# PSUM sums and accumulating DMAs in the second product of an MLP by Strassen-Winograd

## The chip, the cores and the metric

One core of a Trainium2 chip runs the kernel. The metric is the device time of one execution in microseconds (us); the median of several runs is given. The engines are TensorE (PE, with its weight loads PEld), VectorE (DVE), ScalarE (ACT), GpSimd (POOL) and SyncE (SP), which issues the DMAs before the change. SBUF is the on-chip memory, PSUM the memory in which TensorE accumulates, in banks of 128 x 512 float32.

## The reference

A trunk of two layers over x, 1024 tokens of 1024 channels, float32. Each layer has a token mixer (layer 0 a recurrent block, layer 1 a pooling mixer) and an MLP, both gated and modulated by a conditioning vector c:

```python
for i in range(DEPTH):
    sh_m, sc_m, gt_m, sh_f, sc_f, gt_f = split(silu(c) @ w_mod[i] + b_mod[i])
    x = x + gt_m * mixer_i(rms_norm(x) * (1 + sc_m) + sh_m)
    h = rms_norm(x) * (1 + sc_f) + sh_f
    u = relu(h @ w1[i])                  # 1024 -> 4096
    x = x + gt_f * ((u * u) @ w2[i])     # 4096 -> 1024
return rms_norm(x)
```

## The kernel before

The channels lie on the partitions, eight blocks of 128, and the tokens in two halves of 512: `x[h][:, k, :]` is block k of half h, in SBUF (`xa`, `xb` in the profile). Every product is made of three matmuls of 128 x 128 by 128 x 512 (`mm3`, lines 178 to 180): both operands are split into a high and a low part, which add up to float32.

The MLP of a layer runs in eight chunks of 512 hidden channels. `f1` makes a chunk's hidden channels: eight products of 24 matmuls, each followed by relu and square on ScalarE, casts there and subtractions on VectorE. `f2_fast` makes the second product, from Winograd's form of Strassen's method: W2.T is cut into two by two blocks for each of four row blocks r (rows r and r + 4 of the output), the hidden channels into two by two as well, and seven products of six matmuls replace eight. Their operands are sums: of weights, made by `f2_weights` on VectorE one row block ahead (raw tile `raw_w`; parts `w_a_a`, `w_a_s`, `w_s_s`, `w_s`), and of hidden channels (`t1` to `t4`, `ut` in the profile).

`f2_fast` is called whole for twelve chunks: 0 to 5 of layer 0 and 1 to 6 of layer 1, which are written (i, c) here. Chunk (0,6) calls it twice with part of the products, (1, 5, 6, 3, 7) and (2, 4). The rest of the chunks uses the ordinary product, `f2_block`.

What becomes of the products of row block r, with g the gate's column, and the four blocks of the output named by (row, half):

- 1 goes to all four. `S.copy` (line 789) brings it to SBUF (`c1`), and `scaled` (line 774, ScalarE) makes g x product 1, which GpSimd adds to (0,0) (`add_scaled`, line 779).
- 5 goes by `add` (line 770, VectorE, out of PSUM) to (0,1) and (1,1), 2 to (0,0), 3 to (0,1), 4 to (1,0).
- 6 is added to `c1` by VectorE (line 800); ScalarE scales the sum (line 774), GpSimd adds it to (0,1).
- 7 is added on top (line 804), scaled, and added by GpSimd to (1,0) and (1,1).

So a row block has 7 operations on VectorE, 4 on ScalarE and 4 on GpSimd, 52 row blocks with the four of chunk (0,6).

Each product has its own PSUM bank from a pool of six (`acc_mm`), so the bank of a product comes free for the sixth after it. Work tiles (`tmp`) circulate in seven buffers, raw weights in three, split weights in eight. Instructions of an engine run in the order of its queue; a scheduler decides that order when the kernel is built, and waits between engines are set by the data. In layer 0 a step of the conditioning (`drip`, line 197: a product of a loaded tile `mb` with `cond` on VectorE) is taken with each unit of weights.

Of the kernel before, what the change touches and what calls it, by code (L numbers as in the profile page):

```python
# [15 lines left out]
P = 128  # L16
# [10 lines left out]
W = PAD + H  # L27

# Columns of the packed per-channel vectors, eight columns (one per block of channels) each.
# [13 lines left out]
def trunk_kernel(ctx, tc, xT, vecs, wmod, w_k, w_in, w_y, w_g, w_out, w_p, w1, w2, outT):  # L43
# [16 lines left out]
    class Blocks:  # L60
        """Eight blocks of channels of one half of the tokens, in two slots"""
# [41 lines left out]
    # The weights of the first products, in the order in which they are used: two blocks of rows  # L103
    # of six blocks of the input projection, and the conditioning's blocks of columns.
    mod_raw, k_raw = {}, []

    def piece(r, q, part):
        """Columns of a part of r, which is halved for the first two blocks of rows."""
        n = r.shape[-1] // (2 if q == 0 else 1)
        return part * n, part * n + n  # L110
# [29 lines left out]
    # silu(c) as a row on every partition  # L140
    cs = const.tile([P, NB], F32, name="cs")
    with tc.issue_after(S.activation(cs, vcol("c"), AF.Sigmoid).ins):
        # has the table of the first norm's square root loaded ahead of it
        S.activation(const.tile([P, 1], F32, name="early"), eps, AF.Sqrt)
# [3 lines left out]
    for n in range(2):  # L148
        ps = small_ps()
        # the columns of cs on diagonals, whose sums over the partitions are on every partition  # L150
# [23 lines left out]
    def mm3(ps, unit, col, rh, rl, first, last):  # L174
        """ps += unit[:, col:col+128].T @ (rh + rl)"""
        w, c = unit[col // H], col % H
        wh = w[:, 0, c:c + P]
        PE.matmul(out=ps, lhsT=wh, rhs=rh, start=first, stop=False)  # L178
        PE.matmul(out=ps, lhsT=wh, rhs=rl, start=False, stop=False)  # L179
        PE.matmul(out=ps, lhsT=w[:, 1, c:c + P], rhs=rh, start=False, stop=last)  # L180

    def proj(unit, hh, hl):
        """One 128-row block of W.T @ h for one token half, K = 1024."""
# [11 lines left out]
    def mod_column(m, e, raw):  # L195
        """m[:, e] = raw @ cond"""
        V.scalar_tensor_tensor(raw, raw, 1.0, cond, op0=ALU.mult, op1=ALU.mult, accum_out=m[:, e:e + 1])  # L197
# [8 lines left out]
    def mod_steps():  # L206
        """The rest of the conditioning in small steps, taken between those of the other work."""
# [19 lines left out]
    def norm_scale(g, m, name):  # L227
        """g * (1 + scale)"""
# [5 lines left out]
    class SumSq:  # L234
        """Sums of squares of n tokens: up to three partial sums, added up by the tensor engine."""
# [19 lines left out]
    def rstd_bcast(ss, trace=None):  # L255
        """PSUM tile [P, n] with 1/sqrt(mean + eps) of every token on every partition."""
# [10 lines left out]
        # in two float32r parts on diagonals, whose sums over the partitions are on every partition  # L267
# [38 lines left out]
    # Six blocks of the input projection take the channels of the first half of the tokens  # L306
    # as the conditioning of each 128 of them is ready.
# [8 lines left out]
    def after(f, *args, **kw):  # L316
        """Issues behind what the last call on the same engine issued."""
# [7 lines left out]
    def column(dst, j, k, scale, first):  # L325
        """dst[:, k] = first + scale * (conditioning of channel block k)"""
# [16 lines left out]
    def prepare(q, part=0):  # L343
        """The float32r parts of the weights of two blocks of rows, or of one if q is 0"""
# [126 lines left out]
    # coefficient of the gate in log a: 8 * log_sigmoid(lambda)  # L471
# [17 lines left out]
    # log1p(z) = 2 s (1 + po)  # L489
# [11 lines left out]
    def gates(hd, unit, h):  # L501
        """RG-LRU of one head; its states take the place of its input."""
# [16 lines left out]
        for mi in range(2):  # L519
            b = 2 * hd + mi  # L520
            # a = exp(log a);  1 - a^2 = (1 + a^2) * tanh(-log a)
# [77 lines left out]
    # U[c]: the hidden channels of chunk c, in slots of two blocks each: (first or last two blocks,  # L599
    # half of the tokens), and the sums of them that the second product of the MLP takes  # L600
# [3 lines left out]
    def f1_block(unit, j, h, u, fast):  # L604
# [7 lines left out]
        def minus(a, n):  # L612
            """a less a block that is there in its two parts"""
# [15 lines left out]
        # for f2_fast the halves of the tokens change places  # L629
# [33 lines left out]
    class Ahead:  # L663
        """Units of weights, which are prepared one ahead of those in use"""
# [11 lines left out]
    # pieces of the conditioning by unit of a chunk of the MLP  # L676
# [35 lines left out]
    def f2_weights(i, c, r, eng=None):  # L712
        """The parts of blocks of rows r and r + 4 of W2.T for f2_fast, by the product that takes them"""
# [399 lines left out]
```

## Time and profile of the kernel before

| | |
|---|---|
| median of 3 runs (1795.46 to 1798.61) | 1798.42 us |
| the profiled execution: its span | 1797.3 us |
| TensorE busy | 1718.5 us, 96% |
| VectorE | 1419.8 us, 79% |
| ScalarE | 913.7 us, 51% |
| GpSimd | 585.9 us, 33% |
| DMA queues | one, hardware_dynamic: 157.43 MB, 26.9% of 16 engines' span; two of instructions below 1% |

Only the span is known of the profiled execution, and the rows below have their times from its start. A row of a timeline gives the start, the duration, the engine, the line, the operation with what it writes and reads, and behind "[" the idle time of the engine ahead of it and what ended it. Matmuls overlap: one lasts 0.39 us and the next starts 0.23 us after it did. VectorE's operations overlap a little as well. Lines in the profile are those of the kernel before; the first lines of the changed kernel's functions lie 3 to 16 further down.

### The profile page before, as it was taken

The numbers are of one execution on the slowest core, as the hardware profiler recorded it, in microseconds if no ns is written. First come the engines' busy times: TensorE is split into PE (matmuls) and PEld (weight loads), VectorE is DVE, ScalarE is ACT, GpSimd is POOL, SyncE is SP. The second block draws the span as 40 slices with busy tenths as digits, with TensorE's granted clock in tenths as the row PEclk, the third lists the DMA queues.
The fourth block names the chain that finished last, engine by engine and source line by source line (L and its number), as shares of the span: only waits on it lengthen the run. The fifth ranks groups of instructions, "written<-read, shape, count | busy, mean of one in ns | idle before, by whom it ended". The sixth has DMA issues, their size and how long they took to land.

```text
span 1797.3 us, 20872 instructions
## 1 busy us (share of the span) xinstructions
PE 1718.5 (96%) x7510; PEld 1405.2 (78%) x7510; DVE 1419.8 (79%) x2124; ACT 913.7 (51%) x1558; POOL 585.9 (33%) x434
## 2 busy tenths in 40 slices
PE   6899989989999999999999988999999999999997
PEld 4687768778788888888888766788887787878787
DVE  8997866678888889898876897958787878686836
ACT  4588884255454444545454464445444444545422
POOL 5323341242322414151324655511322324041403
PEclk8999989989999999999999988999999999999999
DMA  9223314521424233242213221231202111121202
GB/s 363 73 84 109 136 47 142 162 83 59 136 70 134 73 115 106 94 126 73 83 58 106 81 72 59 83 105 51 70 33 71 36 59 52 42 61 46 71 13 94
DMA packets 47479, 158.76 MB, mean 88 GB/s; under 512 B 5008, under 2 KB 7440, under 8 KB 47376
## 3 DMA queue, kind: packets, MB, share of 16 engines
q1 hardware_dynamic: 47376, 157.43, 26.9%
q8 instruction: 59, 0.97, 0.2%
q14 instruction: 44, 0.36, 0.1%
HBM read 153.21 MB, written 4.19 MB: 88 GB/s over the span
## 4 chain that ended last, share of the span: by engine, by line
PE 62%; DVE 22%; ACT 5%; issue 5%; DMA 4%; POOL 2%; DVEq 0%; SPq 0%; ACTq 0%; POOLq 0%
PE mm L178 20%; PE mm L179 20%; PE mm L180 20%; DMA mb<-in_wmod 3%; DVE mb L197 2%; DVE xa L770 1%; DVE mw L323 1%; POOL xa L779 1%; DVE pw L900 1%; DVE xb L770 1%; DVE xca L439 1%; PE sm L262 1%; DVE hl L291 1%; DVE w_a_s L171 1%; DVE xcb L439 1%
## 5 line engine op out<-in xcount | busy, mean ns | idle before, releaser
L178 PE MATMUL mm<-hh,w_w 128*128 128x512 f32 x1024 | 401.4, 392 | 0.9 <-DVE xa L770 0.9
L180 PE MATMUL mm<-hh,w_w 128*128 128x512 f32 x1024 | 400.9, 392 | 0.0
L179 PE MATMUL mm<-hl,w_w 128*128 128x512 f32 x1024 | 400.6, 391 | 0.0
L779 POOL TENSOR_TENSOR xb<-xb,c 128x512 f32<-128x512 f32 x104 | 150.4, 1446 | 632.1 <-ACT c L774 564.4
L178 PEld LDWEIGHTS mm<-hh,w_w 128*128 128x128 f32 x1024 | 193.5, 189 | 42.8 <-DVE xa L770 2.7
L180 PEld LDWEIGHTS mm<-hh,w_w 128*128 128x128 f32 x1024 | 193.6, 189 | 40.3
L179 PEld LDWEIGHTS mm<-hl,w_w 128*128 128x128 f32 x1024 | 193.5, 189 | 40.0
L779 POOL TENSOR_TENSOR xa<-xa,c 128x512 f32<-128x512 f32 x104 | 160.3, 1542 | 145.1 <-ACT c L774 145.1
L774 ACT ACTIVATE c<-c,mod 128x512 f32<-128x512 f32 x104 | 75.3, 724 | 209.7 <-DVE c L800 119.8
L197 DVE SCALAR_TENSOR_TENSOR mb<-mb,cond 128x1024 f32<-128x1024 f32 x80 | 113.8, 1423 | 55.2 <-DMA mb<-in_wmod 54.6
L620 ACT ACTIVATE relu<-mm 128x512 f32<-128x512 f32 x128 | 76.2, 595 | 152.4 <-PE mm L180 143.6
L170 ACT CAST w_w<-raw_w 128x512 fp32r<-128x512 f32 x192 | 113.5, 614 | 63.2 <-PE mm L180 50.6
L171 DVE TENSOR_TENSOR w_w<-raw_w,w_w 128x512 fp32r<-128x512 f32 x136 | 130.5, 967 | 16.8 <-ACT w_w L170 16.7
L770 DVE SCALAR_TENSOR_TENSOR xa<-mm,mod,xa 128x512 f32<-128x512 f32 x156 | 112.9, 741 | 16.6 <-POOL xa L779 16.6
L171 POOL TENSOR_TENSOR w_w<-raw_w,w_w 128x512 fp32r<-128x512 f32 x56 | 83.5, 1498 | 71.6 <-ACT w_w L170 62.6
L179 PE MATMUL mm<-u,w_w 128*128 128x512 f32 (+1 forms) x224 | 81.4, 363 | 1.7 <-DVE u L610 1.7
L178 PE MATMUL mm<-u,w_w 128*128 128x512 f32 (+1 forms) x224 | 80.8, 364 | 1.7 <-ACT u L609 1.7
L180 PE MATMUL mm<-u,w_w 128*128 128x512 f32 (+1 forms) x224 | 81.0, 362 | 0.0
L178 PE MATMUL mm<-u,w_a_a 128*128 128x512 f32 x200 | 79.1, 396 | 1.9 <-DVE xa L770 1.0
L610 DVE TENSOR_TENSOR u<-usq,u 128x512 fp32r<-128x512 f32 x102 | 72.9, 715 | 8.5 <-ACT u L609 7.5
L770 DVE SCALAR_TENSOR_TENSOR xb<-mm,mod,xb 128x512 f32<-128x512 f32 x104 | 77.0, 741 | 2.6 <-PE mm L180 2.2
L179 PE MATMUL mm<-u,w_a_a 128*128 128x512 f32 x200 | 78.0, 390 | 0.0
(332 smaller groups left out, 4078.3 us busy)
## 6 DMA issues: line engine op xcount, KB each, us to landing
raw_w<-in_w SPq DMA_DIRECT2D x148, 512.0 KB, 3.6
mb<-in_wmod SPq DMA_DIRECT2D x80, 512.0 KB, 3.6
mw<-in_wmod SPq DMA_DIRECT2D x16, 512.0 KB, 9.6
raw_in<-in_w_in SPq DMA_DIRECT2D x8, 512.0 KB, 3.7
raw_y<-in_w_y SPq DMA_DIRECT2D x8, 512.0 KB, 3.6
raw_o<-in_w_out SPq DMA_DIRECT2D x8, 512.0 KB, 3.7
outT<-o SPq DMA_DIRECT2D x12, 256.0 KB, 2.4
xa<-in_xT SPq DMA_DIRECT2D x4, 512.0 KB, 5.4
```

The costliest lines, as they stand in the source:

```text
L170: S.copy(w[:, 0, 0:n], raw)
L171: (eng or V).tensor_sub(w[:, 1, 0:n], raw, w[:, 0, 0:n].bitcast(F32))
L178: PE.matmul(out=ps, lhsT=wh, rhs=rh, start=first, stop=False)
L179: PE.matmul(out=ps, lhsT=wh, rhs=rl, start=False, stop=False)
L180: PE.matmul(out=ps, lhsT=w[:, 1, c:c + P], rhs=rh, start=False, stop=last)
L197: V.scalar_tensor_tensor(raw, raw, 1.0, cond, op0=ALU.mult, op1=ALU.mult, accum_out=m[:, e:e + 1])
L439: V.scalar_tensor_tensor(o, xr[:, k:k + H], vcol(f"cw{k}", m), o, op0=ALU.mult, op1=ALU.add)
L610: eng.tensor_sub(u[n][:, 1, jj, :], src, u[n][:, 0, jj, :].bitcast(F32))
L620: S.activation(r, ps, AF.Relu)
L770: V.scalar_tensor_tensor(xb, ps, g[:, r + 4 * row:r + 4 * row + 1], xb, op0=ALU.mult, op1=ALU.add)
L774: S.activation(t, src, AF.Identity, scale=g[:, r + 4 * row:r + 4 * row + 1])
L779: G.tensor_add(xb, xb, t)
```

## The change

Products that go to the same outputs are summed in PSUM. In a row block, product 2 is accumulated onto the bank of 1, product 3 onto that of 5, and product 7 onto that of 6, without clearing it. The bank is read once before the second product (1, 5 and 6 are needed alone) and once after it. So a row block uses four banks in place of seven.

- Product 1: ScalarE scales it twice out of PSUM, by the gate of row 0 and of row 1 (tiles `c1[r][0]`, `c1[r][1]`). No copy.
- Product 5 is added to (1,1) only; when 3 has been accumulated onto it, 5 + 3 goes to (0,1).
- Product 6: VectorE makes g0 x 6 + `c1[r][0]` (line 815); 6 + 7 then makes g1 x (6 + 7) + `c1[r][1]` (line 820). Both are scaled already.
- 1 + 2 goes to (0,0), as `add` of product 2.

The scaled sums reach x by `nc.gpsimd.dma_start(xb, t, accum_op=ALU.add)` (line 788), a DMA of 128 x 512 from SBUF to SBUF that adds onto its destination: three for a row block, 144 in all. The two partial calls of chunk (0,6) share banks (3 onto 5, 7 onto 6) and keep GpSimd's additions (line 790), 16 in all. In row blocks 1 to 3 of the whole calls the order of the products is 1, 5, 6, 4, 3, 7, 2, in row block 0 it stays 1, 5, 6, 3, 7, 2, 4.

```diff
-        def product(parts, n):
-            ps = acc_mm()
+        def product(parts, n, onto=None):
+            ps = acc_mm() if onto is None else onto
             w, c0, ops = parts[n]
             for k in range(2):
-                mm3(ps, [w], c0 + k * P, u[ops][:, 0, k, :], u[ops][:, 1, k, :], k == 0, k == 1)
+                mm3(ps, [w], c0 + k * P, u[ops][:, 0, k, :], u[ops][:, 1, k, :],
+                    onto is None and k == 0, k == 1, True)
             return ps
...
         def add_scaled(t, r, row, col):
             xb = x[1 - col][:, r + 4 * row, :]
-            G.tensor_add(xb, xb, t)
+            if whole:
+                nc.gpsimd.dma_start(xb, t, accum_op=ALU.add)
+            else:
+                G.tensor_add(xb, xb, t)
...
-            ps = product(units[r], n)
+            ps = banks[r, n] = product(units[r], n, banks.get((r, {2: 1, 3: 5, 7: 6}.get(n))))
             if n == 1:
-                c1[r] = tmp("c1")
-                S.copy(c1[r], ps)
-                add_scaled(scaled(ps, r, 0), r, 0, 0)
+                c1[r] = [scaled(ps, r, row) for row in (0, 1)]
+                if not whole:
+                    add_scaled(c1[r][0], r, 0, 0)
+                    c1[r][0] = c1[r][0], tmp("c")
             elif n == 2:
                 add(ps, r, 0, 0)
             elif n == 5:
-                add(ps, r, 0, 1)
                 add(ps, r, 1, 1)
             elif n == 3:
                 add(ps, r, 0, 1)
+                if whole:
+                    add_scaled(c1[r][0], r, 0, 1)
             elif n == 6:
-                w = w16[r] = c1[r]
-                V.tensor_add(w, ps, c1[r])
-                add_scaled(scaled(w, r, 0), r, 0, 1)
+                src, w = (c1[r][0], c1[r][0]) if whole else c1[r][0]
+                V.scalar_tensor_tensor(w, ps, gate(r, 0), src, op0=ALU.mult, op1=ALU.add)
+                if not whole:
+                    add_scaled(w, r, 0, 1)
             elif n == 7:
-                w = w16[r]
-                V.tensor_add(w, ps, w)
-                c = scaled(w, r, 1)
-                add_scaled(c, r, 1, 0)
-                add_scaled(c, r, 1, 1)
+                w = c1[r][1]
+                V.scalar_tensor_tensor(w, ps, gate(r, 1), w, op0=ALU.mult, op1=ALU.add)
+                if (r, 4) in banks or not whole:
+                    add_scaled(w, r, 1, 0)
+                add_scaled(w, r, 1, 1)
             else:
                 add(ps, r, 1, 0)
+                if whole and (r, 7) in banks:
+                    add_scaled(c1[r][1], r, 1, 0)
...
-            for n in products:
+            for n in products if r == 0 or not whole else (1, 5, 6, 4, 3, 7, 2):
                 step(r, n)
```

The scheduler puts the instructions in a new order at three places of which the prediction speaks. `mm_...` are PSUM banks by product, `ut2` and `ut4` are the operands of products 6 and 4, `u11` that of 3.

TensorE, chunk (1,2), row block 0, where product 6 ends and product 3 begins; before:

```order
L179 MATMUL mm_10573<-ut2_10213,w_s2_s4_10453 128x512
L180 MATMUL mm_10573<-ut2_10213,w_s2_s4_10453 128x512
L178 MATMUL mm_10584<-u11_10209,w_s2_s4_10453 128x512
L179 MATMUL mm_10584<-u11_10209,w_s2_s4_10453 128x512
L180 MATMUL mm_10584<-u11_10209,w_s2_s4_10453 128x512
```

The same place after, lines 181 to 183 being `mm3`:

```order
L182 MATMUL mm_10295<-ut2_9937,w_s2_s4_10177 128x512
L183 MATMUL mm_10295<-ut2_9937,w_s2_s4_10177 128x512
L181 MATMUL mm_10326<-ut4_9939,w_a22_s1_10174 128x512
L181 MATMUL mm_10287<-u11_9933,w_s2_s4_10177 128x512
L182 MATMUL mm_10287<-u11_9933,w_s2_s4_10177 128x512
```

Product 3 now goes to mm_10287, the bank of product 5, and one matmul of product 4 (mm_10326) stands ahead of it; the other five come after product 2. It is so in ten of the twelve whole calls. In chunk (0,0) all of product 2 and one matmul of 4 stand there, in chunk (1,1) four matmuls of product 2.

VectorE at the same place, from the last operands of `f1` (L610) on; before:

```order
L171 TENSOR_TENSOR w_s3_10549<-raw_w2_1_2_1_10534,w_s3_10549 128x256
L610 TENSOR_TENSOR u10_10211<-usq_10527,u10_10211 128x512
L770 SCALAR_TENSOR_TENSOR xa_0_81<-mm_10564,mod1_5_6290,xa_0_81 128x512
L610 TENSOR_TENSOR ut4_10215<-udiff_10490,ut4_10215 128x512
L770 SCALAR_TENSOR_TENSOR xa_1_82<-mm_10564,mod1_5_6290,xa_1_82 128x512
L800 TENSOR_TENSOR c1_10559<-mm_10573,c1_10559 128x512
```

After, where L613 is what was L610 and L778 what was L770:

```order
L171 TENSOR_TENSOR w_s3_10273<-raw_w2_1_2_1_10258,w_s3_10273 128x256
L613 TENSOR_TENSOR u10_9935<-usq_10251,u10_9935 128x512
L778 SCALAR_TENSOR_TENSOR xa_1_82<-mm_10287,mod1_5_6110,xa_1_82 128x512
L613 TENSOR_TENSOR ut4_9939<-udiff_10214,ut4_9939 128x512
L815 SCALAR_TENSOR_TENSOR c_10283<-mm_10295,mod1_5_6110,c_10283 128x512
L778 SCALAR_TENSOR_TENSOR xa_0_81<-mm_10287,mod1_5_6110,xa_0_81 128x512
```

The first read of product 5 keeps its place, the second has gone, and the last row reads 5 + 3 out of the shared bank.

VectorE, the same chunk, from the last subtraction for row block 3 on; before:

```order
L171 TENSOR_TENSOR w_s3_10721<-raw_w2_1_2_3_10706,w_s3_10721 128x256
L770 SCALAR_TENSOR_TENSOR xa_0_81<-mm_10736,mod1_5_6290,xa_0_81 128x512
L770 SCALAR_TENSOR_TENSOR xa_1_82<-mm_10736,mod1_5_6290,xa_1_82 128x512
L800 TENSOR_TENSOR c1_10731<-mm_10745,c1_10731 128x512
L171 TENSOR_TENSOR w_w1_1_3_0_0_10794<-raw_w1_1_3_0_10792,w_w1_1_3_0_0_10794 128x512
L770 SCALAR_TENSOR_TENSOR xa_0_81<-mm_10756,mod1_5_6290,xa_0_81 128x512
L804 TENSOR_TENSOR c1_10731<-mm_10764,c1_10731 128x512
```

After:

```order
L171 TENSOR_TENSOR w_s3_10427<-raw_w2_1_2_3_10412,w_s3_10427 128x256
L778 SCALAR_TENSOR_TENSOR xa_1_82<-mm_10441,mod1_5_6110,xa_1_82 128x512
L815 SCALAR_TENSOR_TENSOR c_10437<-mm_10449,mod1_5_6110,c_10437 128x512
L778 SCALAR_TENSOR_TENSOR xb_1_84<-mm_10457,mod1_5_6110,xb_1_84 128x512
L171 TENSOR_TENSOR w_w1_1_3_0_0_10491<-raw_w1_1_3_0_10489,w_w1_1_3_0_0_10491 128x512
L778 SCALAR_TENSOR_TENSOR xa_0_81<-mm_10441,mod1_5_6110,xa_0_81 128x512
```

The addition of product 4 (xb_1_84) has come ahead of the subtraction of the next chunk's weights (w_w1), and product 3 is read with 5 out of one bank, mm_10441.

## Rows read from the trace of the kernel before

**Rows 1.** Stretches: length; PE, PEld, DVE, ACT, POOL busy us (count); PEclk; DMA share; GB/s.

```profile
440.00:520.00 80.00, 78.08 (x341) 63.45 (x340) 68.72 (x112) 38.42 (x68) 22.46 (x15) 1.00 0.34 109
1320.00:1400.00 80.00, 78.97 (x348) 64.77 (x347) 62.73 (x91) 37.19 (x67) 22.61 (x16) 1.00 0.17 53
```

**Rows 2.** Waits of weight loads (us in total, times, longest), whole execution.

```profile
PEld mm L178 <- DVE xa L770: 13.6, 17, 1.4
```

**Rows 3.** Timeline of PE (start, us, ..., idle before) around waits in five chunks.

```profile
455.19 0.50 PE L178 MATMUL mm<-u,w_a_a 128*128 128x512 f32 x1 [1.00 <-DVE xa L770]
...
466.37 0.50 PE L178 MATMUL mm<-hh,w_w 128*128 128x512 f32 x1 [0.92 <-DVE xa L770]
...
545.75 0.50 PE L178 MATMUL mm<-u,w_a_a 128*128 128x512 f32 x1 [0.20 <-DVE xb L770]
...
792.70 0.50 PE L178 MATMUL mm<-u,w_a_a 128*128 128x512 f32 x1
...
1352.87 0.39 PE L180 MATMUL mm<-ut,w_a_s 128*128 128x512 f32 x1
1354.25 0.50 PE L178 MATMUL mm<-ut,w_s_s 128*128 128x512 f32 x1 [0.99 <-DVE xa L770]
...
1687.12 0.50 PE L178 MATMUL mm<-ut,w_s_s 128*128 128x512 f32 x1 [0.99 <-DVE xa L770]
```

**Rows 4.** Timeline of VectorE before the wait that ends at 1354.25.

```profile
1347.35 1.52 DVE L171 TENSOR_TENSOR w_s<-raw_w,w_s 128x256 fp32r<-128x256 f32 x1
...
1352.15 1.39 DVE L171 TENSOR_TENSOR w_w<-raw_w,w_w 128x512 fp32r<-128x512 f32 x1 [1.36 <-ACT w_w L170]
1353.46 0.74 DVE L770 SCALAR_TENSOR_TENSOR xa<-mm,mod,xa 128x512 f32<-128x512 f32 x1
```

**Rows 5.** Timeline of ScalarE there.

```profile
1350.88 0.72 ACT L774 ACTIVATE c<-c,mod 128x512 f32<-128x512 f32 x1 [3.66 <-DVE c L800]
```

**Rows 6.** Timelines of PE, then VectorE, first row block of that chunk.

```profile
1324.21 0.39 PE L178 MATMUL mm<-ut,w_s_s 128*128 128x512 f32 x1
...
1325.57 0.39 PE L178 MATMUL mm<-u,w_s_s 128*128 128x512 f32 x1
...
1324.04 0.42 DVE L171 TENSOR_TENSOR w_s<-raw_w,w_s 128x256 fp32r<-128x256 f32 x1
1324.38 0.69 DVE L610 TENSOR_TENSOR u<-usq,u 128x512 fp32r<-128x512 f32 x1
1324.98 0.75 DVE L770 SCALAR_TENSOR_TENSOR xa<-mm,mod,xa 128x512 f32<-128x512 f32 x1
```

**Rows 7.** The same of chunk (0,0): PE, then VectorE.

```profile
429.55 0.39 PE L178 MATMUL mm<-u,w_s_s 128*128 128x512 f32 x1
...
429.52 1.78 DVE L616 TENSOR_TENSOR udiff<-udiff,ut 128x512 f32<-128x512 f32 x1
...
431.56 0.74 DVE L770 SCALAR_TENSOR_TENSOR xa<-mm,mod,xa 128x512 f32<-128x512 f32 x1
```

**Rows 8.** The same of chunk (1,1): PE, then VectorE.

```profile
1243.92 0.39 PE L178 MATMUL mm<-u,w_s_s 128*128 128x512 f32 x1
...
1244.89 0.74 DVE L770 SCALAR_TENSOR_TENSOR xa<-mm,mod,xa 128x512 f32<-128x512 f32 x1
```

**Rows 9.** The same of chunk (0,6), fourth row block.

```profile
945.38 0.39 PE L178 MATMUL mm<-u,w_a_s 128*128 128x512 f32 x1
...
947.69 0.75 DVE L770 SCALAR_TENSOR_TENSOR xa<-mm,mod,xa 128x512 f32<-128x512 f32 x1
```

**Rows 10.** Page, part 5 (busy us, mean ns, idle before and releaser): conditioning steps.

```profile
L197 DVE SCALAR_TENSOR_TENSOR mb<-mb,cond 128x1024 f32<-128x1024 f32 x80 | 113.8, 1423 | 55.2 <-DMA mb<-in_wmod 54.6
```

**Rows 11.** Page, part 6 (count, KB each, median us to landing): DMA issues.

```profile
raw_w<-in_w SPq DMA_DIRECT2D x148, 512.0 KB, 3.6
mw<-in_wmod SPq DMA_DIRECT2D x16, 512.0 KB, 9.6
outT<-o SPq DMA_DIRECT2D x12, 256.0 KB, 2.4
```

More of the change, by code (lines that the diff above doesn't have):

```diff
@@ L172, in split_part, with mm3 @@
         return w
-    def mm3(ps, unit, col, rh, rl, first, last):
+    def mm3(ps, unit, col, rh, rl, first, last, shared=False):
         w, c = unit[col // H], col % H
         wh = w[:, 0, c:c + P]
-        PE.matmul(out=ps, lhsT=wh, rhs=rh, start=first, stop=False)
-        PE.matmul(out=ps, lhsT=wh, rhs=rl, start=False, stop=False)
-        PE.matmul(out=ps, lhsT=w[:, 1, c:c + P], rhs=rh, start=False, stop=last)
+        PE.matmul(out=ps, lhsT=wh, rhs=rh, start=first, stop=False, skip_group_check=shared)
+        PE.matmul(out=ps, lhsT=wh, rhs=rl, start=False, stop=False, skip_group_check=shared)
+        PE.matmul(out=ps, lhsT=w[:, 1, c:c + P], rhs=rh, start=False, stop=last, skip_group_check=shared)
     def proj(unit, hh, hl):
@@ L759, in f2_fast, with gate @@
         u, g = U[c], mod[i, 5]
-        def product(parts, n):
-            ps = acc_mm()
+        def product(parts, n, onto=None):
+            ps = acc_mm() if onto is None else onto
             w, c0, ops = parts[n]
             for k in range(2):
-                mm3(ps, [w], c0 + k * P, u[ops][:, 0, k, :], u[ops][:, 1, k, :], k == 0, k == 1)
-            return ps
+                mm3(ps, [w], c0 + k * P, u[ops][:, 0, k, :], u[ops][:, 1, k, :],
+                    onto is None and k == 0, k == 1, True)
+            return ps
+        def gate(r, row):
+            return g[:, r + 4 * row:r + 4 * row + 1]
         def add(ps, r, row, col):
             xb = x[1 - col][:, r + 4 * row, :]
-            V.scalar_tensor_tensor(xb, ps, g[:, r + 4 * row:r + 4 * row + 1], xb, op0=ALU.mult, op1=ALU.add)
+            V.scalar_tensor_tensor(xb, ps, gate(r, row), xb, op0=ALU.mult, op1=ALU.add)
         def scaled(src, r, row):
             t = tmp("c")
-            S.activation(t, src, AF.Identity, scale=g[:, r + 4 * row:r + 4 * row + 1])
+            S.activation(t, src, AF.Identity, scale=gate(r, row))
             return t
@@ L778, in add_scaled @@
             xb = x[1 - col][:, r + 4 * row, :]
-            G.tensor_add(xb, xb, t)
-        units, c1, w16 = {}, {}, {}
+            if whole:
+                nc.gpsimd.dma_start(xb, t, accum_op=ALU.add)
+            else:
+                G.tensor_add(xb, xb, t)
+        units, c1, banks = {}, {}, {}
+        whole = len(products) == 7
         def step(r, n):
```

## The prediction

> **What bounds the kernel now.** I read the busy time of each engine by stretch first, then who made TensorE wait, and last the timelines around those waits. In a whole chunk of layer 1 TensorE is busy 78.97 of 80 us at a granted clock of 1.00, while VectorE has 62.73, ScalarE 37.19 and GpSimd 22.61 [rows 1]. So GpSimd's busy time costs nothing by itself; the change can pay only where TensorE waits. Those waits have one main source in the MLP: weight loads stood 13.6 us, in 17 places, behind VectorE's additions of line 770 [rows 2].
>
> How much they cost: product 6 of a row block starts at 1324.21 and product 3 at 1325.57, so a product of six matmuls takes 1.36 us, a matmul 0.2267, and the 360 matmuls of a chunk 81.6 us [rows 6]. In layer 1 the same wait, idle 0.99 us behind VectorE, ends at 1354.25 and four chunks later at 1687.12 [rows 3]: 332.87 / 4 = 83.2 us a chunk, 1.6 too long, in five chunks **8.0 us**. In layer 0 the likes of the wait that ends at 545.75 come every 82.3 us (792.70 is the third after it, 246.95 / 3) [rows 3]: 0.7 too long, in four chunks 2.8. Chunk 0 idles 1.00 and 0.92 us [rows 3]. At 1354.25 an idle of 0.99 is a step of 1.38 us, 1.15 more than 0.23 [rows 3], so these two cost 2.3. **All that sharing or lightening can give back is 8.0 + 2.8 + 2.3 = 13.1 us.**
>
> Why VectorE is late there: a subtraction of 256 columns with both inputs in SBUF takes 1.52 us at 1347.35, beside a GpSimd addition, and the same kind takes 0.42 at 1324.04 without one [rows 4, 6]. Then it idles 1.36 us for ScalarE's cast [rows 4], and ScalarE had stood 3.66 us at a scaling that waited for VectorE's addition of line 800 [rows 5]. Each waits for the other, over GpSimd's queue. TensorE restarts at 1354.25, 0.05 us after the VectorE addition that frees its bank (1353.46 + 0.74) [rows 3, 4].
>
> **The change, part by part.** (1) *Removed.* 192 of 208 additions on GpSimd go, 22.61 us for 16 of them [rows 1], so 1.41 each and some 270 us off an engine that has slack; with them go the contention and ScalarE's head-of-queue wait, since both scalings now read PSUM when product 1 is ready. On VectorE seven operations a row block become six of the same kind. A row block of 9.52 us (7 x 1.36) then holds six at 0.75 us, five subtractions of 256 columns at 0.42 and three of 512 at 0.69, where each starts some 0.08 before the one ahead of it ends (1324.04 and 0.42 against 1324.38) [rows 6]: 8.7 - 1.1 = 7.6 us. In layer 0 a conditioning step of 1.42 us joins it [rows 10], so 9. In a row-by-row schedule with uncontended durations no step waits from row block 1 on: products 3 and 7 have one or two products (1.36 to 2.72 us) between the bank's first use and the second. I take the 13.1 us as gone; bounds 8 (only layer 1 gains) and 13.1.
>
> (2) *Added: a bank used twice.* In row block 0 product 3 follows product 6 directly and adds onto 5's bank, so TensorE waits for VectorE's read of product 5. In the chunk at 1321.49 that read starts 1324.98 and ends 1325.73; product 3 started 1325.57 [rows 6]. With the 0.05 of the restart it would lose 0.21 us, in ten chunks 2.1. But the new order runs one matmul of product 4 before it, 0.23 us of work that was due anyway, and that covers the 0.21. Cost 0 to 0.21 a chunk; I take 0.05, **0.5 us** in all. What it needs, the operand cast on ScalarE, is there by then; if it were late the cover is gone and the 2.1 are paid.
> Chunk (0,0): the read stood at 431.56, product 3 at 429.55, and 1.78 of the subtraction ahead of it are the price of a GpSimd addition beside it (the two-input kind takes 0.69 alone) [rows 6, 7]. Without that the read ends near 431.2, 1.7 late; the order puts product 2 and one matmul of 4 (7 x 0.2267 = 1.6) ahead. **0.3 us** (0 to 1.2).
> Chunk (1,1): the read of 5 starts 1244.89 and ends 1245.64, product 3 was at 1243.92 [rows 8], 1.77 late with the restart; four matmuls of product 2 fill 0.91. **1.0 us** (0.5 to 1.9).
> Chunk (0,6) keeps its GpSimd additions in four row blocks of 6.8 us, and shares banks all the same. In the last of them product 3 started at 945.38 and VectorE's reads of product 5 at 947.69 [rows 9], behind a wait for GpSimd. Left as late as that, the four would cost 7.5; VectorE is one addition a block lighter and reads 5 earlier in the first block, and walking the new order through with the same durations leaves 0.15 + 0.5 + 0.6 + 1.2 = **2.5 us** (0.5 to 7).
> In layer 0 a conditioning step stands between the reads in some row blocks. It waits on its DMA 55.2 us over 80 steps, 0.7 each [rows 10], with about 1 us of slack. **0.5 us** (0 to 3).
>
> (3) *Added: 144 accumulating DMAs of 256 KB from SBUF to SBUF.* No row before shows such a transfer. The nearest are the store of 256 KB (2.4 us from issue to landing), the load of 512 KB (3.6) and the loads of the crowded start (9.6) [rows 11]. Nobody adds onto the same block for most of a chunk afterwards, so latency alone is free. What waits is the buffer: seven temporaries circulate, and the fourth relu of the next chunk, 4 x 5.44 = 21.8 us in, needs those of the last row block. Twelve transfers have from the first (some 5 us into the 38 us of products) until then, about 54 us: 4.5 us each if they ran strictly one behind another. I take 2.4 to 3.6, which hides, so 0 us; above 4.5 the excess of all twelve lands on ScalarE's relu and on TensorE.
> The Trainium skill ("DMA: Bandwidth & Descriptors", Anatomy of one DMA — SWDGE (gpsimd) path) fits 2.0 us + bytes / 436e3 per DMA issued from GpSimd; 256 KB gives an estimate of 2.6 us, and by it the term is also 0. No run here shows one yet.
>
> **Sum.** -13.1 + 0.5 + 0.3 + 1.0 + 2.5 + 0.5 = -8.3 us on the profiled span of 1797.3, so 1789.0. The median of the runs is 1798.42, 1.1 above that span, so 1790.1.
>
> **Rivals.**
> *No change* (1795 to 1802): the new waits eat the gain. This is the case if the fillers don't fill (2.1 + 1.7 + 1.8), chunk (0,6) costs 6 and the conditioning steps 1.5: 13.1 - 13.1 = 0, so 1798. For it: every one of these waits is on an engine that ran late before, and in row block 0 VectorE is late with the last operands of the first product, which nothing in the change shortens. Against: the order shows work placed in each of those gaps.
> *All of it* (below 1788): bounds of 0 everywhere but (0,6), 13.1 - 2.5, so 1787.8 and less, to 1786 with (0,6) at 0.5.
> *Slower, by the transfers* (above 1802): the accumulating DMA reads its destination as well as its source, and takes 5 us or more in series. From 4.5 us it decides: at 5 us, 12 x 0.5 = 6 us a chunk, 72 over twelve chunks, and some 1860; at 4.8, 43 less 8, some 1833. For it: loads already fill 0.34 of the DMA engines in layer 0 [rows 1], and nothing of this kind was ever in flight. Against: 3.6 us for twice the bytes [rows 11].
> Its second form: GpSimd, which issues them, is held up while VectorE works, since a two-input operation of VectorE already takes three times as long when both run [rows 4, 6].
> The Trainium skill ("SBUF — State Buffer", Who interferes with whom) says that GpSimd writes the descriptors of such a DMA and starves while VectorE runs copies, casts or scalar operations in a two-port mode, and infers that tensor-tensor operations leave it alone. VectorE's rows here are two-tensor or fused operations, so by that page the second form would not appear; no row before shows it either way.
> *Slower, by the shared banks* (1802 to 1810): from row block 1 on, VectorE falls more than 1.4 us behind in layer 0, where 9 of 9.5 us are work, and products 3 and 6 wait in every block. It decides from 8.3 / 12 = 0.7 us a chunk beyond the sum: 0.8 in each of the 24 row blocks of layer 0 would be 19, less 8, so 1809.
>
> **How the numbers follow.** About 0.2% (3.6 us: 1794.8 and 1802.0) is what a measurement of this kernel tells from no change. Forecast 0.52; all of it 0.08; no change 0.22; slower by transfers 0.11; by banks 0.07. Faster 0.60, same 0.22, slower 0.18. The range leaves out the two slower cases and the upper end of no change: 1786 to 1800.
>
> **What would show it.** Right: the steps at 1354 and its four likes are 0.23 us; GpSimd has 16 additions left and transfers of 2.4 to 3.6 us; a step of under 0.35 before product 3 in row block 0, about 1 us in (1,1), and two to three us in (0,6); ScalarE's relu never waits for a transfer. Wrong: relu or VectorE rows released by a DMA onto x; steps over 0.5 us in row blocks 1 to 3 of layer 0; weight loads that land later than 3.6 us.

## The result and the profile after

The changed kernel takes 1813.7 us (1808.38 to 1814.19, 4 runs) where the kernel before takes 1798.35: a ratio of 1.0084, 95% interval 1.0067 to 1.0101. It is **slower by 15 us**; forecast were 1790.1, in a range of 1786 to 1800. The profiled run is the one of 1808.38, so the traces below show a loss of 9.3 us (span 1806.6 against 1797.3), not of 15; where the other 6 go is told with the second profile of it below (a2).

Page of the changed kernel, parts 1, 3, 5 and 6 (columns as in the rows of before).

```profile
PE 1716.8 (95%) x7510; PEld 1405.3 (78%) x7510; DVE 1298.0 (72%) x2072; ACT 862.4 (48%) x1454; POOL 428.6 (24%) x386
...
q1 hardware_dynamic: 47376, 157.43, 27.0%
q0 software_dynamic: 20736, 37.76, 12.1%
...
L200 DVE SCALAR_TENSOR_TENSOR mb<-mb,cond 128x1024 f32<-128x1024 f32 x80 | 104.7, 1310 | 92.1 <-DMA mb<-in_wmod 92.1
...
raw_w<-in_w SPq DMA_DIRECT2D x148, 512.0 KB, 3.8
...
xa<-c POOLq DMA_DIRECT2D x96, 256.0 KB, 5.9
xb<-c POOLq DMA_DIRECT2D x48, 256.0 KB, 5.6
```

VectorE lost 122 us of work, ScalarE 51, GpSimd 157, and the kernel is slower. Two lines are out of place. The 80 conditioning steps (L200, the L197 of before) now stand 92.1 us behind their loads, where it was 54.6 [rows 10]. The transfers take 5.9 and 5.6 us, not 2.4 to 3.6.

Windows of the changed kernel, in a whole chunk of layer 0 and in one of layer 1, and then the first window of the kernel before.

```profile
520.00:600.00 80.00, 76.93 (x340) 63.16 (x338) 57.86 (x102) 34.29 (x60) 9.66 (x11) 1.00 0.53 137
1320.00:1400.00 80.00, 80.00 (x354) 66.09 (x353) 52.48 (x88) 35.01 (x61) 10.52 (x12) 1.00 0.39 88
```

```profile
520.00:600.00 80.00, 79.80 (x351) 65.57 (x350) 68.94 (x109) 39.07 (x69) 23.07 (x16) 1.00 0.32 102
```

Layer 1 is as forecast: TensorE 80.00 of 80, where it was 78.97 [rows 1]. In the window of layer 0 it idles 3.07 us, where the kernel before idles 0.20. The granted clock is 1.00 in all three, so this is waiting.

To account for the whole I add up, over TensorE's matmuls, what each start-to-start step has beyond 0.2255 us (a matmul that waits for nothing starts about that long after the one ahead of it), where the step is over 0.28. I call this the excess of a stretch (us, stretches by the time from the span's start):

| stretch | before | changed | e1, below |
|---|---|---|---|
| up to 425 | 60.4 | 62.6 | 59.4 |
| 425 to 1000, MLP of layer 0 | 5.8 | **21.5** | 3.1 |
| 1000 to 1240 | 33.8 | 32.7 | 32.8 |
| 1240 to 1740, MLP of layer 1 | 7.8 | **0.5** | 0.5 |

The change gained 7.3 us in layer 1 and lost 15.7 in layer 0. Waits of TensorE in the changed kernel, the longest group (line waiting, what released it: us in total, times, longest):

```profile
PE mm L181 <- DVE c L815: 13.8, 5, 3.4
```

L815 is VectorE's read of product 6. Five times TensorE waits for it, at the first matmul of product 7, which accumulates onto the bank that L815 reads: idle 3.07 us at 549.37, 3.29 at 634.84, 3.38 at 720.26, 3.16 at 807.22 and 0.93 at 464.27. It is always row block 3 of a whole chunk, in chunks 0 to 4 of layer 0. Chunk 5, where no conditioning step stands there, has no such wait. The place at 549 in the timelines of the changed kernel (columns as before), TensorE first:

```profile
545.91 0.39 PE L183 MATMUL mm<-u,w_s_s 128*128 128x512 f32 x1
549.37 0.50 PE L181 MATMUL mm<-ut,w_s 128*128 128x512 f32 x1 [3.07 <-DVE c L815]
```

The same of VectorE:

```profile
538.92 1.23 DVE L200 SCALAR_TENSOR_TENSOR mb<-mb,cond 128x1024 f32<-128x1024 f32 x1 [2.07 <-DMA mb<-in_wmod]
...
543.85 0.74 DVE L778 SCALAR_TENSOR_TENSOR xa<-mm,mod,xa 128x512 f32<-128x512 f32 x1
547.42 1.23 DVE L200 SCALAR_TENSOR_TENSOR mb<-mb,cond 128x1024 f32<-128x1024 f32 x1 [2.82 <-DMA mb<-in_wmod]
548.57 0.08 DVE L200 DVE_READ_ACCUMULATOR mb<-mb,cond 128x1 f32 x1
548.57 0.75 DVE L815 SCALAR_TENSOR_TENSOR c<-mm,mod,c 128x512 f32<-128x512 f32 x1
```

The same of SyncE's queue, which issues the loads, and then of GpSimd, which issues the transfers:

```profile
542.10 0.33 SPq L215 DMA_DIRECT2D mb<-in_wmod  x1
```

```profile
541.22 0.89 POOL L788 DMA_DIRECT2D xa<-c  x1 [9.42 <-DVE xa L778]
541.88 1.13 POOL L788 DMA_DIRECT2D xb<-c  x1
542.42 1.48 POOL L788 DMA_DIRECT2D xa<-c  x1
```

Read from the bottom. Three transfers go out from 541.22 on; the load of `mb` goes out among them at 542.10 and the step that needs it starts at 547.42, 5.3 us later. VectorE's conditioning step stands for it 2.82 us, works 1.15, and only then comes L815, whose bank holds product 6, finished before the wait began. L815 ends at 549.32 and TensorE restarts 0.05 later. In the kernel before the two stood the other way round. VectorE's timeline there, the read of 6 and then the step:

```profile
548.56 0.67 DVE L800 TENSOR_TENSOR c<-mm,c 128x512 f32<-128x512 f32 x1
549.16 1.21 DVE L197 SCALAR_TENSOR_TENSOR mb<-mb,cond 128x1024 f32<-128x1024 f32 x1
```

So two things came together: an instruction with a wait that stands in the queue ahead of one that TensorE now depends on, and a load that takes longer.

### The profile page after: what moved, and what is told of

Same layout as the page of the kernel before. It is cut to its first block, busy times and chain, and to the rows that moved or that the text cites. A ratio compares the mean times of both kernels' runs of the same rounds, so it can differ in the third digit from the quotient of the medians.

```text
span 1806.6 us, 20695 instructions
## 1 busy us (share of the span) xinstructions
PE 1716.8 (95%) x7510; PEld 1405.3 (78%) x7510; DVE 1298.0 (72%) x2072; ACT 862.4 (48%) x1454; POOL 428.6 (24%) x386
## 3 DMA queue, kind: packets, MB, share of 16 engines
q1 hardware_dynamic: 47376, 157.43, 27.0%
q0 software_dynamic: 20736, 37.76, 12.1%
## 4 chain that ended last, share of the span: by engine, by line
PE 68%; DVE 17%; DMA 7%; ACT 4%; issue 3%; POOL 1%; SPq 0%; DVEq 0%; ACTq 0%; POOLq 0%
PE mm L181 22%; PE mm L182 22%; PE mm L183 22%; DMA mb<-in_wmod 6%; DVE mb L200 2%; DVE mw L326 1%; DVE pw L918 1%; DVE xca L442 1%; DVE hl L294 1%; DVE xcb L442 1%; PE sm L265 1%; DVE pl L933 1%; DVE nt L287 1%; POOL asq L531 1%; DVE gate L532 1%
## 5 line engine op out<-in xcount | busy, mean ns | idle before, releaser
L788 POOL DMA_DIRECT2D xa<-c x96 | 97.4, 1015 | 850.2 <-DVE xa L778 768.8
L170 ACT CAST w_w<-raw_w 128x512 fp32r<-128x512 f32 x192 | 118.5, 620 | 208.6 <-PE mm L183 131.9
L200 DVE SCALAR_TENSOR_TENSOR mb<-mb,cond 128x1024 f32<-128x1024 f32 x80 | 104.7, 1310 | 92.1 <-DMA mb<-in_wmod 92.1
L778 DVE SCALAR_TENSOR_TENSOR xa<-mm,mod,xa 128x512 f32<-128x512 f32 x104 | 77.7, 747 | 35.3 <-PE mm L183 30.0
L171 DVE TENSOR_TENSOR w_w<-raw_w,w_w 128x512 fp32r<-128x512 f32 x136 | 95.5, 709 | 7.4 <-ACT w_w L170 7.4
L778 DVE SCALAR_TENSOR_TENSOR xb<-mm,mod,xb 128x512 f32<-128x512 f32 x104 | 77.6, 747 | 14.9 <-PE mm L183 14.4
L782 ACT ACTIVATE c<-mm,mod 128x512 f32<-128x512 f32 x104 | 67.3, 687 | 34.8 <-PE mm L183 34.8
L613 DVE TENSOR_TENSOR u<-usq,u 128x512 fp32r<-128x512 f32 x102 | 73.0, 715 | 8.3 <-ACT u L612 7.3
L181 PE MATMUL mm<-u,w_a_a 128*128 128x512 f32 x200 | 78.2, 391 | 0.0
L182 PE MATMUL mm<-u,w_a_a 128*128 128x512 f32 x200 | 78.0, 390 | 0.0
L183 PE MATMUL mm<-u,w_a_a 128*128 128x512 f32 x200 | 77.8, 389 | 0.0
```

Source lines behind the costliest of these rows:

```text
L170: S.copy(w[:, 0, 0:n], raw)
L171: (eng or V).tensor_sub(w[:, 1, 0:n], raw, w[:, 0, 0:n].bitcast(F32))
L181: PE.matmul(out=ps, lhsT=wh, rhs=rh, start=first, stop=False, skip_group_check=shared)
L182: PE.matmul(out=ps, lhsT=wh, rhs=rl, start=False, stop=False, skip_group_check=shared)
L613: eng.tensor_sub(u[n][:, 1, jj, :], src, u[n][:, 0, jj, :].bitcast(F32))
L778: V.scalar_tensor_tensor(xb, ps, gate(r, row), xb, op0=ALU.mult, op1=ALU.add)
```

## The experiments

Two theories went in. The first, A in the expectations: the order of VectorE's queue is the cause, a conditioning step with its wait ahead of the read of 6. Against it stand the rivals that the transfers themselves are the cause (B), or the shared banks. Ratios are to the kernel before, timed beside each kernel on the same chip, with their 95% interval. Line numbers move by 2 or 3 between these kernels: L780 and L778 are `add`, L812 to L817 the read of 6.

### The step behind the read of 6 (e1, and again e1b)

```diff
-                mod_column(m, e, raw)
+                with tc.issue_after(sixth[-1].ins) if sixth else nullcontext():
+                    mod_column(m, e, raw)
...
-                V.scalar_tensor_tensor(w, ps, gate(r, 0), src, op0=ALU.mult, op1=ALU.add)
+                sixth.append(V.scalar_tensor_tensor(w, ps, gate(r, 0), src, op0=ALU.mult, op1=ALU.add))
```

> The changed kernel; every conditioning step (line 200) is issued behind the VectorE read of product 6 (line 815 in the changed kernel) that was traced last, instead of ahead of it. Nothing else changes. Theory A (the order): TensorE loses 3.1 to 3.4 us at product 7 of the fourth row block of each chunk of layer 0, since that read stands in VectorE's queue behind a conditioning step that waits for its load. Then these five stalls fall below 0.5 us each, layer 0 gives back 14 to 17 us, and the time is 1792 to 1799. Theory B (the transfers): the accumulating DMAs make the loads late and VectorE late with them whatever the order; then the stall moves to another product of the same row block, at least 8 of the 16 us stay, and the time is above 1802.

1787.03 against 1795.12: 0.9952 (0.9938 to 0.9967). That is below the range of theory A, which had counted on 14 to 17 us of layer 0; its excess fell by 18.4. The same kernel a second time:

> The kernel of e1 again, beside the other two on the same chip: 1785 to 1789, 9 to 12 us below the kernel before.

1788.09 against 1798.85: 0.9937 (0.9921 to 0.9953). Window of e1, the same chunk of layer 0:

```profile
520.00:600.00 80.00, 80.00 (x355) 66.03 (x354) 60.67 (x106) 34.22 (x60) 10.33 (x12) 1.00 0.54 142
```

TensorE no longer waits, with the same transfers and the same DMA share (0.54 against 0.53). The loads that mattered are not any quicker. Those of the five steps that had stalled TensorE took 5.2 to 5.6 us from issue to landing in the changed kernel, and the same five (counted in order of issue) take 6.5 to 7.6 in e1. VectorE stands for them 1.6 to 2.7 us there, but behind the read of 6, and TensorE has no wait at product 7. So for these five the order alone decides whether a late load costs anything. The edit also changes how the other loads fall: VectorE stands for 15 loads between 440 and 920 us, not for 30. From issue to the start of the waiting step they take 6.7 us with a transfer issued near (median of 10), and 3.5 without (5). What is left in layer 0 stands in chunk (0,6). Waits of e1:

```profile
PE mm L181 <- DVE xa L780: 1.4, 2, 0.9
```

### The steps on data that is there (e7)

```diff
-                nc.sync.dma_start(raw, wmod[i, j, e])
-                mod_column(m, e, raw)
+                if i == 0:
+                    nc.sync.dma_start(raw, wmod[i, j, e])
+                    mod_column(m, e, raw)
+                else:
+                    V.scalar_tensor_tensor(raw, cond, 1.0, cond, op0=ALU.mult, op1=ALU.mult, accum_out=m[:, e:e + 1])
```

> The changed kernel, in which the conditioning steps of layer 1 do the same work on VectorE at the same place, on data that is in SBUF; their loads are left out (and with them layer 1's conditioning has no meaning). Here two steps stand ahead of the read of product 6 in the fourth row block, where there was one. Theory A by the load: with nothing to wait for, 2.4 us of work fit into the 2.5 us between products 6 and 7, the stalls of 3.1 to 3.4 us fall below 1 us each, and the time is 1787 to 1795. Theory A by the work: the step itself makes the read late, stalls of 1 to 2.5 us stay in each chunk, and the time is 1798 to 1808.

1784.14 (2 runs) against 1799.07: 0.9918 (0.9894 to 0.9942), some 3 us below the range of theory A by the load. VectorE's timeline shows a step (here L219) two places ahead of the read of 6 (L818), and nothing waits:

```profile
537.39 1.23 DVE L219 SCALAR_TENSOR_TENSOR mb<-cond 128x1024 f32<-128x1024 f32 x1
538.55 0.08 DVE L219 DVE_READ_ACCUMULATOR mb<-cond 128x1 f32 x1
538.55 0.75 DVE L781 SCALAR_TENSOR_TENSOR xa<-mm,mod,xa 128x512 f32<-128x512 f32 x1
539.21 0.75 DVE L818 SCALAR_TENSOR_TENSOR c<-mm,mod,c 128x512 f32<-128x512 f32 x1
```

TensorE's excess in layer 0's MLP is 3.4 us, and it has no wait at product 7. So it is the wait for the load, not the step's 1.2 us of work.

### No transfers (e10)

```diff
             if whole:
-                nc.gpsimd.dma_start(xb, t, accum_op=ALU.add)
+                pass
```

> The changed kernel with the 144 accumulating DMAs left out (the scaled sums with products 6 and 7 never reach x); its order on VectorE is unchanged, the conditioning step directly ahead of the read of product 6 in the fourth row block, and no transfer flies beside the loads. In the changed kernel the loads of conditioning steps took 5.3 to 5.7 us from issue there, against 3.5 where no transfer was near. If both the order and the slow load count, the load lands some 1.9 us sooner, the stalls of 3.1 to 3.4 us at product 7 shrink to 1.0 to 1.8 us and the time is 1792 to 1800. If the order alone makes them, they stay above 2.5 us and the time above 1804. If the slow load alone does, they fall below 0.5 us and the time below 1791.

1792.07 against 1798.43: 0.9967 (0.9955 to 0.9978). The order is that of the changed kernel. Timelines of TensorE, then VectorE, at the place that was at 549:

```profile
544.11 0.50 PE L181 MATMUL mm<-ut,w_s 128*128 128x512 f32 x1 [0.49 <-DVE c L815]
```

```profile
534.74 1.23 DVE L200 SCALAR_TENSOR_TENSOR mb<-mb,cond 128x1024 f32<-128x1024 f32 x1 [0.57 <-DMA mb<-in_wmod]
...
542.16 1.23 DVE L200 SCALAR_TENSOR_TENSOR mb<-mb,cond 128x1024 f32<-128x1024 f32 x1 [1.74 <-DMA mb<-in_wmod]
```

The time is in the range for both causes together, but the stalls are shorter than the 1.0 to 1.8 us expected there: idle 0.49 to 0.85 us (0.8 to 1.1 lost) in place of 3.07 to 3.38. The loads that VectorE stood for took 4.3 us to the start of the step (median of 24). So of the 12.9 us that the four long stalls idle, roughly four fifths come from loads slowed beside transfers, and a fifth (2.8) from the order with loads as they are without transfers.

At the first of these places one can follow how two slow loads add up. Without transfers the load takes 4.1 us and not 5.2, which is 1.1 of the 2.6 us between the two stalls. The other 1.5 come from the step before it: VectorE stands for that one's load 0.57 us and not 2.07, so the next load goes out 1.5 us earlier, counted back from where product 7 was due. Neither theory alone would do: with the order mended (e1) or the load left out (e7) the stall goes whole.

### One half of the change at a time (e2, e3)

PSUM sums, with GpSimd's additions kept:

```diff
-            if whole:
-                nc.gpsimd.dma_start(xb, t, accum_op=ALU.add)
-            else:
-                G.tensor_add(xb, xb, t)
+            G.tensor_add(xb, xb, t)
```

> The changed kernel with GpSimd additions in place of the accumulating DMAs: PSUM sums alone. VectorE's order at the fourth row block is as in the changed kernel, the conditioning step ahead of the read of product 6. Theory A: the five stalls of layer 0 stay at 1.5 to 3.3 us each (the load lands up to 1.6 us sooner without the transfers), layer 1 keeps most of its gain, and the time is 1798 to 1810. Theory B: the loads land in 3.6 to 3.8 us again, the stalls fall below 1 us each, and the time is 1788 to 1796.

1808.26 against 1795.12: 1.0071 (1.0056 to 1.0086). As slow, but in another way: the time is in the range of theory A, whose stalls at product 7 are not what makes it. TensorE's timeline shows waits at product 3, here of 0.78 us, and of 1.56 in the next row block:

```profile
537.70 0.50 PE L181 MATMUL mm<-u,w_s_s 128*128 128x512 f32 x1 [0.78 <-DVE xa L778]
```

and in its timeline VectorE, which is to read product 5 for it, is behind:

```profile
532.62 2.32 DVE L200 SCALAR_TENSOR_TENSOR mb<-mb,cond 128x1024 f32<-128x1024 f32 x1
...
536.90 0.74 DVE L778 SCALAR_TENSOR_TENSOR xa<-mm,mod,xa 128x512 f32<-128x512 f32 x1
```

The step takes 2.32 us beside GpSimd's additions, 1.23 without (e10). The loads that VectorE stood for took 4.0 us (median of 25, to the start of the step). Shared banks need a VectorE that is on time, and GpSimd's additions take that away.

The accumulating transfers alone, for all 208 additions of the kernel before:

```diff
-            G.tensor_add(xb, xb, t)
+            nc.gpsimd.dma_start(xb, t, accum_op=ALU.add)
```

> The kernel before (seven banks a row block, its order of products) with accumulating DMAs in place of all 208 GpSimd additions, four a row block. Theory A: a late read of product 6 blocks no product for six more, so the conditioning steps cost TensorE nothing, VectorE is free of GpSimd's additions, and the time is 1784 to 1793. Theory B: 208 transfers instead of 144 delay loads more; TensorE or VectorE waits in layer 0 grow beyond those of the changed kernel, and the time is above 1805.

1819.7 against 1795.12: 1.0141 (1.0122 to 1.016). Theory B had the time, but what it gave as the reason, later loads, was not the main one: VectorE stands 26.8 us for loads of conditioning steps between 440 and 920, against 21.3 in the kernel before. VectorE's waits of e3 in layer 0 (440 to 920):

```profile
DVE xb L770 <- DMA xb<-c: 35.8, 18, 5.2
DVE xa L770 <- DMA xa<-c: 29.9, 18, 3.5
```

In the order of before five additions of VectorE and four of GpSimd go to the same four blocks of x within a row block, so VectorE's next addition has to wait for the transfer to land. In the same stretch of the kernel before it stood 11.8 us for GpSimd. Transfers took 4.8 and 5.1 us here. TensorE's excess in layer 0's MLP is 28.5 us. With the PSUM sums there are seven writes to x a row block and not nine, and in the changed kernel VectorE waits for no transfer onto x. So each half of the change loses alone.

### With the order mended, are the transfers worth it? (e5)

e1 with GpSimd's additions, the edit as in e2.

> The kernel of e1 (every conditioning step behind the read of product 6) with GpSimd additions in place of the accumulating DMAs. Theory A (with VectorE's order mended, the transfers are what keeps VectorE on time): GpSimd's additions slow VectorE's two-input operations again, the waits of 0.8 and 1.4 to 1.6 us at product 3 in row blocks 2 and 3 of the first run of PSUM sums alone stay in layer 0, and the time is 1795 to 1804. Theory C (the transfers are worth nothing, the order was all): those waits go as well, and the time is 1785 to 1790.

1796.92 against 1799.07: 0.9988 (0.9979 to 0.9998). Against e1's two ratios the transfers are worth some 6 to 9 us. Each whole chunk of layer 0 waits at product 3. Timelines of TensorE, and of VectorE ahead of it:

```profile
525.79 0.50 PE L181 MATMUL mm<-u,w_s_s 128*128 128x512 f32 x1 [0.57 <-DVE xa L780]
```

```profile
522.16 1.52 DVE L724 TENSOR_TENSOR raw_w<-raw_w 128x256 f32<-128x256 f32 x1
523.71 0.42 DVE L726 TENSOR_TENSOR raw_w<-raw_w 128x256 f32<-128x256 f32 x1
```

Two operations of one kind and size, 1.52 us beside a GpSimd addition and 0.42 without: the same price as in [rows 4, 6]. The waits are in the places that were expected, but shorter (about 0.6 us, in one row block).

### The edit of e1 on the kernel before (e9)

The same wrapping, on the read of 6 at line 800.

> The kernel before with the edit of e1 alone: every conditioning step behind the read of product 6 (line 800). Theory A: with seven banks a row block the step's place blocks no product, so the edit alone is worth less than 3 us either way, 1794 to 1801. Rival: the step's place is worth as much there as in the changed kernel (over 8 us), and e1 owes its time to the edit alone, 1787 to 1790.

1796.85 against 1798.85: 0.9990 (0.9981 to 1.0000). So e1's gain is not the edit's by itself: where the step stood behind the read already, it is worth about 2 us (0 to 3.4 by the interval).

### The changed kernel again (a2)

> The changed kernel again, beside the others on the same chip: 1808 to 1814, five stalls of 3 us at product 7 in layer 0.

1813.82 against 1799.07: 1.0085 (1.0070 to 1.0100). The profiled run took 1813.73 (span 1812.0), so it shows what the one of 1808.38 does not. Timeline of TensorE, and the window around it:

```profile
545.22 0.40 PE L183 MATMUL mm<-u,w_s_s 128*128 128x512 f32 x1
549.33 0.80 PE L181 MATMUL mm<-ut,w_s 128*128 128x512 f32 x1 [3.71 <-DVE c L815]
549.92 0.63 PE L182 MATMUL mm<-ut,w_s 128*128 128x512 f32 x1
550.35 0.63 PE L183 MATMUL mm<-ut,w_s 128*128 128x512 f32 x1
```

```profile
545.00:555.00 10.00, 6.29 (x16) 4.64 (x15) 6.45 (x11) 1.38 (x3) 2.41 (x3) 0.66 0.87 220
```

After an idle of 3.71 us the matmuls start 0.43 apart, not 0.23, 1.2 GHz in place of 2.4 (mean granted clock 0.66 in these 10 us); it is so again after an idle of 4.68 at 811.87. Each time 12 to 15 matmuls go at that level, 0.2 us dearer each, some 2.5 to 3 us. So these two stalls cost 1.6 to 1.8 times their length. A third one in a2, of 3.06 us, is followed by some six such steps. Its row of the timeline, and a window behind it, with a granted clock of 0.50:

```profile
637.38 0.79 PE L181 MATMUL mm<-ut,w_s 128*128 128x512 f32 x1 [3.06 <-DVE c L815]
```

```profile
637.50:640.30 2.80, 2.80 (x7) 2.22 (x8) 2.35 (x4) 0.00 (x0) 0.65 (x1) 0.50 0.86 289
```

In the first profile only the stall at 807.22 (3.16 us) is followed by such steps, some seven, and those of 3.07, 3.29 and 3.38 by none. So the length of the stall alone does not tell which one is followed by slow matmuls. Layer 0's excess is 28.3 us in a2 and 21.5 in the first profile, and most of that difference, some 5 us, is these slow steps; this is where the 5.4 us between the two spans go.

### Chunk (0,6): the order of its products, and its additions (e6, e8)

e1 with product 5 ahead of product 1 in the first partial call:

```diff
-    f2_fast(0, 6, Ahead([partial(f2_weights_one, 0, 6, r, V) for r in range(4)]), (1, 5, 6, 3, 7))
+    f2_fast(0, 6, Ahead([partial(f2_weights_one, 0, 6, r, V) for r in range(4)]), (5, 1, 6, 3, 7))
```

> The kernel of e1, in which the first partial call of chunk (0,6) takes its products as 5, 1, 6, 3, 7 instead of 1, 5, 6, 3, 7, so that one more product lies between 5 and the product 3 that goes onto its bank. If the read of 5 is what product 3 waits for there (0.58 and 0.87 us in e1, with what follows 1.9 us), the waits fall to 0 to 0.5 and the span by 1 to 2 us, the time 1784 to 1787. If GpSimd's additions hold VectorE up as a whole, nothing changes by more than 0.5 us.

1788.02 against 1799.07: 0.9938 (0.9921 to 0.9955), no difference from e1. The waits of TensorE show the same two places as in e1, 1.5 us in all:

```profile
PE mm L181 <- DVE xa L780: 1.5, 2, 0.9
```

So it is not the time between 5 and 3. VectorE's timeline in e1 names what it is:

```profile
938.02 0.75 DVE L780 SCALAR_TENSOR_TENSOR xa<-mm,mod,xa 128x512 f32<-128x512 f32 x1 [2.44 <-POOL xa L792]
```

L792 is the GpSimd addition onto the same block of x, of which these calls kept 16. e8 is e1 with transfers there too:

```diff
-            if whole:
-                nc.gpsimd.dma_start(xb, t, accum_op=ALU.add)
-            else:
-                G.tensor_add(xb, xb, t)
+            nc.gpsimd.dma_start(xb, t, accum_op=ALU.add)
...
-                if whole:
-                    add_scaled(c1[r][0], r, 0, 1)
+                add_scaled(c1[r][0], r, 0, 1)
...
-                if not whole:
-                    add_scaled(w, r, 0, 1)
+                c1[r][0] = w
```

> The kernel of e1, in which the first partial call of chunk (0,6) uses accumulating DMAs too, four a row block, that of the sum with product 6 issued behind VectorE's addition onto the same block. GpSimd has no additions left in the second product. If its additions hold VectorE up there, the two waits of 0.6 and 0.9 us at product 3 (1.9 us with what follows) go, and the time is 1.5 to 2.5 us below e1 beside it. If the transfers cost as much there, it is within 1 us of e1.

1785.45 against 1798.85: **0.9924** (0.9909 to 0.9939), 2.6 us below e1b, timed with it on one chip. The two intervals overlap, so the gain over e1b rests on the traces, where layer 0's excess goes from 3.1 us to 0.9. Windows of chunk (0,6) of e1b, then of e8 (columns as in [rows 1]):

```profile
915.00:955.00 40.00, 38.49 (x169) 30.98 (x168) 30.89 (x42) 18.63 (x32) 23.67 (x16) 1.00 0.26 80
```

```profile
915.00:955.00 40.00, 40.00 (x178) 33.01 (x177) 26.34 (x42) 19.19 (x33) 13.94 (x16) 1.00 0.86 195
```

TensorE has no wait of over 0.5 us left in layer 0's MLP, and that with DMA engines at 0.86: there, where no conditioning step waits for a load, busy DMA engines cost TensorE nothing. e8 is faster than both kernels.

## Why the prediction was wrong

The forecast was faster by 8.3 us; measured is slower by 15. One term, put at 0.5 us, cost 18 us in one profile and 25 in the other (layer 0's excess of 21.5 and 28.3 beyond the 3.1 of e1, which differs by the place of the steps).

- *What bounds the kernel, and the 13.1 us to be had*: right. The 7.8 us of layer 1 went to 0.5, and with the order mended layer 0 went from 5.8 to 3.1, new waits included. e1 gains 8.1 and 10.8 us in its two measurements, against the 8.3 of the sum.
- *Row block 0, ten chunks, 0.5 us*: right in kind, 0.9 in size. One step of 0.31 or 0.32 us stands in each place, some 0.09 us a chunk, where 0.05 was taken.
- *Chunk (0,0), 0.3 us*: 0.2. *Chunk (1,1), 1.0 us*: 0.09; the fillers cover it.
- *Chunk (0,6), 2.5 us*: about 2.0, idle 0.62 and 0.85 us in the changed kernel, and for the reason given, GpSimd's additions (e8).
- *The conditioning steps, 0.5 us (0 to 3)*: **this is the step that failed.** It took the wait for the load from before, 0.7 us a step on average [rows 10], and set it against about 1 us of slack. The term asked for two things that it didn't look up: behind which instruction the step stands in the new order of VectorE's queue, and how long the load takes beside the transfers. The new order has it directly ahead of the read of 6 in row block 3, and TensorE waits there because of the shared bank. The rows of the new order in the section on the change are of a chunk of layer 1, where no such step stands. Where VectorE stood for a load with a transfer issued near, it took 5.6 us to the start of the step (median of 20, 440 to 920), not 3.6, so that one wait is 2.82 us, not 0.7. TensorE's idle measured 3.2 us in each of four chunks and 0.9 in one, 13.8 together, and 1.49 more at 802.41, where a step stood 3.85 us and put VectorE behind. To that comes the clock (a2).
- *Transfers, 0 us*: wrong in its size and incomplete in what it asks. They took 5.6 and 5.9 us, 1.6 to 2.5 times the 2.4 to 3.6 taken and above the 4.5 named as the point from which ScalarE's relu would wait. That wait came nearly not at all: never in the first profile, and twice, 9.6 us, in a2, where TensorE waited at neither. The 4.5 held for transfers strictly one behind another, and up to three were in flight together: those at 541 were issued within 1.2 us, and the first landed 5.9 us after its issue. The term asked who waits for the transfers; the cost was in what else was in flight. By the Trainium skill ("DMA: Bandwidth & Descriptors", Anatomy of one DMA — SWDGE (gpsimd) path) the estimate was 2.6 us; the trace does not agree, 5.6 and 5.9.
- *Rivals*: the shared banks were the nearest, with VectorE late and TensorE at a bank, and from 0.7 us a chunk it was to decide. It was 3 us a chunk in four of twelve, at product 7 and in one row block, where the rival had products 3 and 6 in every block. The transfers' second form, GpSimd held up by VectorE, did not appear: an issue took 0.86 us in the median where VectorE was busy for most of it (99 issues that did not overlap another), and 0.86 in the two where VectorE was nearly idle.
- *What would show it wrong*: of the three signs named, two came: steps of over 0.5 us in row blocks 1 to 3 of layer 0, and loads that land late (those of the conditioning; the weight loads' median went from 3.6 to 3.8). The third, relu released by a transfer, came in a2 alone of the changed kernel's two profiles, and cost TensorE nothing. Product 7 was not suspected because before, in its own bank, it could not wait for the read of 6.

Left open: why a transfer takes 5.6 to 5.9 us, and by what it slows the loads. With 48 loads fewer (e7) transfers took 5.1 and 3.9, which speaks for each slowing the other; whether they meet at the DMA engines or at the memory no run here tells apart. Also open is why a stall of 3.1 us is followed by slow matmuls in one place and not in another.

## What to carry to other kernels

When a change gives two products one bank, every reader of that bank joins TensorE's path: look in the new order at what stands directly ahead of it in its queue, above all at an instruction that waits for a DMA, and move that behind the reader. Ask of an added transfer not only who waits for it, but which loads fly beside it and who waits for those. A change of two halves can lose by either alone (1.0071, 1.0141) and by both (1.0084), and still gain (0.9952 and 0.9937) when the one queue position that they make matter is put right.

## What the runs showed of the hardware

- An accumulating DMA of 256 KB from SBUF to SBUF, issued by GpSimd: 5.9 and 5.6 us from issue to landing in the changed kernel, 4.8 and 5.1 in e3, 5.1 and 3.9 in e7. Its issue holds GpSimd 1.0 us in the mean (97.4 us for 96), and 0.86 where no other issue overlaps it.
- By the page of the changed kernel the 37.76 MB of these transfers took 12.1% of the DMA engines' time, the 157.43 MB of the other queue 27.0%: a megabyte of an accumulating transfer took 1.9 times as much.
- Loads of 512 KB that VectorE stood for took 5.6 us (changed kernel) and 6.7 (e1) with such a transfer issued near, 3.5 in both without. Not every load beside a transfer is slow: in e1, of 31 loads of the conditioning in flight together with one (440 to 920), 10 took 6.5 to 7.6 us and 21 took 3.3 to 4.5.
- After an idle of 3.71 and of 4.68 us TensorE came back at 1.2 GHz for 12 to 15 matmuls; after idles of 3.07, 3.29 and 3.38 it came back at 2.4, after one of 3.06 (a2) and one of 3.16, with another of 1.49 shortly ahead, at 1.2 for six or seven. So a stall cost up to 1.8 times its length.
